# A layer norm's turn to token-major and back: 32 tensor-engine transposes, or block transposes on VectorE and a trip through HBM

## The chip, the cores and the metric

One core of a Trainium2 chip runs one program. The metric is device time in microseconds (us) of one execution; lower is better. Three runs of the kernel before gave 762.21, 762.23 and 762.68 us, median 762.23. The engines are named as in the profile: PE (tensor engine), DVE (VectorE), ACT (ScalarE), POOL (GpSimd), and SP, whose queue issues most DMAs.

## The reference, cut to what matters

A decoder layer on 512 tokens of width 1024. One of its two branches is a causal convolution over 512 channels; a layer norm and a SiLU follow, then a projection:

```
z = lax.conv_general_dilated(z, rhs, ..., feature_group_count=CONV_CH)   # width 31, depthwise
z = z + conv_b
mu = mean(z, axis=-1); var = mean((z - mu)**2, axis=-1)                  # over the 512 channels
y = (z - mu) * rsqrt(var + EPS) * ln_g + ln_b
conv_out = silu(y) @ w_conv_out
```

Beside it stand the latent attention branch, 16 blocks of gate columns (`gates = sigmoid(...)`), a merge, a cross-attention, an MLP and a last norm. Every product is computed in three matmuls from values split in a high and a low part (`hi`, `lo`).

## The kernel before, in words

Activations lie channel-major: 128 channels on the partitions, 512 tokens along them, so `acc[:, c, :]` (c = 0 to 3) holds the convolution's output. The mean over channels would run across partitions; so the norm turns `acc` to token-major (`ln[:, t, :]`, 128 tokens on the partitions, 512 channels along them), takes sum and squares per partition on ACT (L525, L530), normalises (L537), and turns back. Each turn is 16 PE transposes of 128x128 into PSUM banks, from which ACT reads (L524, L545). The way back ends in a SiLU to `acc` (L546) and the split into `yh` and `yl`, the operands of the projection `conv_out`.

The convolution's 124 taps run on DVE beside PE's matmuls: each group of three matmuls calls `tick`, which emits taps at a set rate. Around the norm PE works through the 16 gate units (`proj_unit`): each has 24 matmuls into one of four PSUM banks named `mm`; DVE then multiplies the bank by `rbx` into a scratch tile (L727) and ACT takes the sigmoid (L728). The scratch tag `sg` has two buffers, and the norm's `junk` tiles have the same tag:

```
junk = wkp.tile([P, S], F32, tag="sg", name="junk")     # in layer_norm_in
t = wkp.tile([P, S], F32, tag="sg", name="sg")          # in evac_gate
```

Weights come in chunks through two `raw` buffers, loaded by SP in the order of use: ..., gate chunk 7 (units 14 and 15), wk, wv, uq0, co0, uq1. `prep` casts a chunk or a half of it on ACT to `wh` (L202) and takes the rest on DVE or POOL to `wl` (L203); the three `wh`/`wl` buffers come free when PE has used them. POOL does it for the gate chunks.

When the convolution's generator ends, the norm isn't emitted at once: `after(D_LN1, ...)` puts its first half 10 ticks later, and `after(D_LN2, ...)` the second half 20 ticks later, each into the stream of the gate matmuls. PE's order is the program's; the other engines' order is set by a scheduler at build time and is then fixed: every engine and SP run their instructions in that order, and a waiting one holds all behind it.

Behind the gate units come, on PE: `k_pair(0)` (6 matmuls), the values `vh`, `vl` (24), `q_head(0)` (9), `q_head(1)` (9), `scores(0)`, `k_pair(1)`, `q_head(2)`, and then `conv_out`, the first reader of `yh`. ACT and DVE turn each of these banks into operands (`k`, `vh`/`vl`, `qtmp`, `q`). `k_pair(0)`'s bank is the one that `q_head(1)` takes next.

A kernel part that stands already in the program uses the operation that the change brings in: `spill`, in the MLP, turns `ht` by a DVE transpose of 32x32 blocks and four DMAs to an HBM tensor `hsp` that set the blocks in place, in runs of 32 floats (128 bytes).

Of the kernel before, what the change touches and what calls it, by code (L numbers as in the profile page):

```python
# [14 lines left out]
F32 = mybir.dt.float32  # L15
# [3 lines left out]
AF = mybir.ActivationFunctionType  # L19
# [4 lines left out]
P = 128  # L24
D = 1024
S = 512
NT = S // P
KD = D // P
CC = 512
CT = CC // P  # L30
# [135 lines left out]
D_LN1, D_LN2, D_R1, D_R2, D_M = 10, 20, 11, 8, 24  # L166


def _body(tc, a):
    nc = tc.nc  # L170
    dma = nc.sync.dma_start
    pe = nc.tensor
    dve = nc.vector
    act = nc.scalar
    gps = nc.gpsimd

    def pool(name, bufs=1, side=None, space=None):
        kw = dict(name=name, bufs=bufs, reuse_waits="tile")
        if side:
            kw["side"] = side  # L180
        if space:
            kw["space"] = space
        cm = tc.tile_pool(**kw)
        return cm, cm.__enter__()
# [11 lines left out]
    def bank(tag="mm"):  # L196
        nonlocal ps
        return ps.tile([P, S], F32, tag=tag, name=tag, bufs=PB[tag])


    def split(hi, lo, src, eng=None):
        act.copy(hi, src)  # L202
        (eng or dve).tensor_tensor(lo, src, hi.bitcast(F32), op=ALU.subtract)  # L203
# [10 lines left out]
    def after(ticks, fn):  # L214
        clock[1] += 1
        heapq.heappush(later, (clock[0] + ticks, clock[1], fn))
# [25 lines left out]
    def rsqrt(dst, v, n):  # L242
        t = sm.tile([P, n], F32, tag="rs_t", name="rs_t")
        ti = sm.tile([P, n], I32, tag="rs_i", name="rs_i")
        dve.tensor_scalar(ti, v.bitcast(I32), 1, None, op0=ALU.logical_shift_right)
        dve.tensor_scalar(dst.bitcast(I32), ti, -1, 0x5F3759DF, op0=ALU.mult, op1=ALU.add)
        for _ in range(3):
            dve.scalar_tensor_tensor(t, dst, -0.5, dst, op0=ALU.mult, op1=ALU.mult)  # L248
            dve.tensor_tensor(t, t, v, op=ALU.mult)
            dve.scalar_tensor_tensor(dst, t, 1.5, dst, op0=ALU.add, op1=ALU.mult)  # L250
# [4 lines left out]
    ident = kon[:, K_ID:K_ID + 128]  # L255
# [8 lines left out]
    def v_(name, i):  # L264
        o = VOFF[name] + i
        return vec[:, o:o + 1]
# [26 lines left out]
    sp_cm, spp = pool("spill", space=bass.MemoryType.DRAM)  # L293
# [94 lines left out]
    acc = b1.tile([P, CT, S], F32, name="acc")  # L388
# [5 lines left out]
    wk_cm, wkp = pool("wk", bufs=2, side="right")  # L394
# [91 lines left out]
    def conv_taps(c):  # L486
        run = bank("cv")
        for w in range(CW):
            zs = zpad[:, c, w:w + S]
            wcol = vec[:, w * CT + c:w * CT + c + 1]  # L490
            if w == 0:
                dve.tensor_scalar(run, zs, wcol, v_("conv_b", c), op0=ALU.mult, op1=ALU.add)
            else:
                dve.scalar_tensor_tensor(run if w < CW - 1 else acc[:, c, :], zs, wcol, run,  # L494
                                         op0=ALU.mult, op1=ALU.add)
            yield

    def conv_gen():

        started, chains = 0, []  # L500
        while started < CT or chains:
            if len(chains) < 2 and started < min(CT, zready[0]):
                chains.append(conv_taps(started))
                started += 1
            if not chains:
                yield False
                continue
            for g in list(chains):
                try:
                    next(g)  # L510
                    yield True
                except StopIteration:
                    chains.remove(g)
        after(D_LN1, layer_norm_in)

    def layer_norm_in():

        ln = tmp_.tile([P, NT, CC], F32, tag="tmaj", name="ln", bufs=1)
        s1 = sm.tile([P, NT], F32, tag="lns1", name="lns1")
        s2 = sm.tile([P, NT], F32, tag="lns2", name="lns2")  # L520
        for t in range(NT):
            b = bank(("at", "cv")[t % 2])
            for c in range(CT):
                pe.transpose(b[:, c * P:(c + 1) * P], acc[:, c, t * P:(t + 1) * P], ident)  # L524
            act.activation(ln[:, t, :], b, AF.Copy, accum_out=s1[:, t:t + 1])  # L525
        nmu = sm.tile([P, NT], F32, tag="lnm", name="lnm")
        dve.tensor_scalar(nmu, s1, -1.0 / CC, None, op0=ALU.mult)
        for t in range(NT):
            junk = wkp.tile([P, S], F32, tag="sg", name="junk")
            act.activation(junk, ln[:, t, :], AF.Square, bias=nmu[:, t:t + 1], accum_out=s2[:, t:t + 1])  # L530
        v = sm.tile([P, NT], F32, tag="rv", name="rv")
        dve.tensor_scalar(v, s2, 1.0 / CC, EPS, op0=ALU.mult, op1=ALU.add)
        r = sm.tile([P, NT], F32, tag="lnr", name="lnr")
        rsqrt(r, v, NT)
        dve.tensor_tensor(nmu, nmu, r, op=ALU.mult)
        for t in range(NT):
            act.activation(ln[:, t, :], ln[:, t, :], AF.Identity, scale=r[:, t:t + 1],  # L537
                           bias=nmu[:, t:t + 1])
        after(D_LN2, lambda: layer_norm_out(ln))

    def layer_norm_out(ln):
        for c in range(CT):
            b = bank(("at", "cv")[c % 2])
            for t in range(NT):
                pe.transpose(b[:, t * P:(t + 1) * P], ln[:, t, c * P:(c + 1) * P], ident)  # L545
            act.activation(acc[:, c, :], b, AF.Silu, scale=v_("conv_ln_g", c),  # L546
                           bias=v_("conv_ln_b", c))
            split(yh[:, c, :], yl[:, c, :], acc[:, c, :])

    conv = conv_gen()  # L550
    taps = [0.0, False]

# [201 lines left out]
    at_cm, at = pool("att", side="right")  # L754
# [87 lines left out]
    for t in range(NT):  # L842
        b = bank(("mm", "at")[t % 2])
# [715 lines left out]
```

## Time and profile before

| what | value |
|---|---|
| median of 3 runs | 762.23 us (762.21 to 762.68) |
| the profiled execution | 762.46 us, of which span 760.7 us |
| PE busy | 745.8 us, 98% of the span |
| DVE, ACT, POOL busy | 529.5 (70%), 388.5 (51%), 80.9 us (11%) |
| norm's first turn on PE (L524) | starts at 157.6 us |
| norm's second turn on PE (L545) | starts at 175.1 us |
| HBM read, written | 94.37 MB, 8.39 MB |

The profiled execution's time is 1.76 us more than its span, and 0.23 us above the median. A row of the timeline gives start, duration, engine, line, operation and out<-in; "xN" means N of them merged, and the bracket the idle time before it and what ended it. The duration of a PE matmul is longer than the distance to the next, since matmuls overlap; the distance is what counts.

### The profile page before, as it was taken

The page shows a single profiled execution, that of the slowest core. Times are in us where ns is not written, and L with a number is a line of the kernel's source. Part 1 is how long each engine was busy: PE and PEld are TensorE (multiplying, and loading weights), DVE is VectorE, ACT ScalarE, POOL GpSimd, SP SyncE. Part 2 cuts the span into 40 slices and gives each one's busy share as a digit, 9 for nine tenths or more (in the row PEclk, how much of TensorE's full clock was granted, in tenths as well). Part 3 has the DMA queues.
Part 4 walks back from the last instruction along what each step waited for, and adds up shares of the span by engine and source line. Part 5 has one row for each costly group of instructions (what it writes and reads, how often), then busy time and mean ns, then how long its engine had stood idle before and what let it go on. Part 6 is the DMA issues. An engine that isn't in the chain of part 4 may idle for free.

```text
span 760.7 us, 9482 instructions
## 1 busy us (share of the span) xinstructions
PE 745.8 (98%) x3562; PEld 620.9 (82%) x3562; DVE 529.5 (70%) x863; ACT 388.5 (51%) x657; POOL 80.9 (11%) x72
## 2 busy tenths in 40 slices
PE   8999899999999999999999999999999999999995
PEld 5889688778788887889888888888888888888884
DVE  6899999845888859856686744333333467677994
ACT  7243334468565637434475544444343566565662
POOL 0144337420000000000000000000000011111000
PEclk9999999999999999999999999999999999999998
DMA  8323124124214144423321536534353499999921
GB/s 270 124 76 133 43 79 163 56 90 139 79 28 139 57 136 151 156 86 137 111 106 61 175 89 190 150 97 184 111 204 106 138 305 263 281 221 214 247 97 56
DMA packets 40302, 105.47 MB, mean 139 GB/s; under 512 B 19264, under 2 KB 22720, under 8 KB 31296
## 3 DMA queue, kind: packets, MB, share of 16 engines
q1 hardware_dynamic: 31648, 73.84, 28.7%
q0 software_dynamic: 2944, 18.88, 12.0%
q10 hardware_dynamic: 5664, 12.15, 4.4%
q8 instruction: 28, 0.46, 0.2%
q14 instruction: 18, 0.15, 0.1%
HBM read 94.37 MB, written 8.39 MB: 135 GB/s over the span
## 4 chain that ended last, share of the span: by engine, by line
PE 79%; DVE 15%; DMA 2%; ACT 2%; issue 1%; SPq 0%; DVEq 0%
PE mm L239 21%; PE mm L237 20%; PE mm L238 20%; DVE cv L494 9%; PE at L239 4%; PE at L238 4%; PE at L237 4%; PE at L817 1%; DMA mtok<-mem 1%; PE at L798 1%; DMA xr<-xT 1%; PE at L799 1%; PE at L796 1%; DVE sg L727 1%; DVE rs_t L248 1%
## 5 line engine op out<-in xcount | busy, mean ns | idle before, releaser
L202 ACT CAST wh<-raw 128x1024 fp32r<-128x1024 f32 (+4 forms) x103 | 102.7, 998 | 170.6 <-PE mm L238 144.7
L203 DVE TENSOR_TENSOR wl<-raw,wh 128x1024 fp32r<-128x1024 f32 (+3 forms) x77 | 90.6, 1177 | 97.7 <-ACT wh L202 97.6
L237 PE MATMUL mm<-hgh,wh 128*128 128x512 f32 x288 | 112.3, 390 | 0.0
L238 PE MATMUL mm<-hgl,wh 128*128 128x512 f32 x288 | 112.1, 389 | 0.0
L239 PE MATMUL mm<-hgh,wl 128*128 128x512 f32 x288 | 112.1, 389 | 0.0
L494 DVE SCALAR_TENSOR_TENSOR cv<-zpad,vec,cv 128x512 f32<-128x512 f32 x116 | 80.4, 741 | 0.1
L237 PE MATMUL mm<-uh,wh 128*128 128x512 f32 x176 | 70.0, 398 | 3.1 <-DVE rr L250 1.6
L239 PE MATMUL mm<-uh,wl 128*128 128x512 f32 x176 | 68.8, 391 | 0.2 <-DVE wl L203 0.2
L238 PE MATMUL mm<-ul,wh 128*128 128x512 f32 x176 | 68.6, 390 | 0.0
L203 POOL TENSOR_TENSOR wl<-raw,wh 128x1024 fp32r<-128x1024 f32 (+2 forms) x26 | 56.5, 2175 | 107.3 <-ACT wh L202 97.0
L239 PEld LDWEIGHTS mm<-hgh,wl 128*128 128x128 f32 x288 | 54.1, 188 | 11.4
L238 PEld LDWEIGHTS mm<-hgl,wh 128*128 128x128 f32 x288 | 54.1, 188 | 11.1
L237 PEld LDWEIGHTS mm<-hgh,wh 128*128 128x128 f32 x288 | 54.1, 188 | 10.9
L203 DVE TENSOR_TENSOR wl<-x,wh 128x1024 fp32r<-128x1024 f32 x25 | 30.4, 1221 | 19.1 <-ACT wh L202 18.3
L1371 POOL COPY paced<-wl 128x1 f32<-128x1 f32 x4 | 2.5, 614 | 385.6 <-DVE wl L203 385.6
L237 PEld LDWEIGHTS mm<-uh,wh 128*128 128x128 f32 x176 | 33.1, 188 | 11.4 <-issue 4.1
L202 ACT CAST wh<-x 128x1024 fp32r<-128x1024 f32 x25 | 26.3, 1051 | 26.6 <-PE mm L238 9.4
L239 PEld LDWEIGHTS mm<-uh,wl 128*128 128x128 f32 x176 | 33.0, 188 | 7.7 <-DVE wl L203 0.7
L238 PEld LDWEIGHTS mm<-ul,wh 128*128 128x128 f32 x176 | 33.1, 188 | 6.4
L237 PE MATMUL at<-wh,hA 128*128 128x512 f32 x96 | 37.4, 389 | 0.0
L238 PE MATMUL at<-wl,hA 128*128 128x512 f32 x96 | 37.4, 389 | 0.0
L239 PE MATMUL at<-wh,hB 128*128 128x512 f32 x96 | 37.4, 389 | 0.0
(397 smaller groups left out, 1701.8 us busy)
## 6 DMA issues: line engine op xcount, KB each, us to landing
raw<-weights SPq DMA_DIRECT2D x42, 1024.0 KB, 4.8
x<-weights POOLq DMA_DIRECT2D x12, 1024.0 KB, 15.3
a<-weights SPq DMA_DIRECT2D x5, 1024.0 KB, 9.0
x<-weights SPq DMA_DIRECT2D x4, 1024.0 KB, 5.0
raw<-weights SPq DMA_DIRECT2D x4, 768.0 KB, 4.4
xr<-xT SPq DMA_DIRECT2D x8, 256.0 KB, 6.3
raw<-weights SPq DMA_DIRECT2D x4, 512.0 KB, 5.1
k<-kr POOLq DMA_DIRECT2D x8, 256.0 KB, 3.7
```

Of the source, the lines that this page charges most:

```text
L202: act.copy(hi, src)
L203: (eng or dve).tensor_tensor(lo, src, hi.bitcast(F32), op=ALU.subtract)
L237: pe.matmul(out, wh, ah, start=first and i == 0, stop=False, **kw)
L238: pe.matmul(out, wh, al, start=False, stop=False, **kw)
L239: pe.matmul(out, wl, ah, start=False, stop=last and i == n - 1, **kw)
L248: dve.scalar_tensor_tensor(t, dst, -0.5, dst, op0=ALU.mult, op1=ALU.mult)
L494: dve.scalar_tensor_tensor(run if w < CW - 1 else acc[:, c, :], zs, wcol, run, op0=ALU.mult, op1=ALU.add)
L727: dve.tensor_tensor(t, b, rbx, op=ALU.mult)
L796: pe.matmul(b[:, :n], q[:, 0, sl], k[:, 0, :n], start=True, stop=False)
L798: pe.matmul(b[:, :n], q[:, 0, sl], k[:, 1, :n], start=False, stop=False)
L799: pe.matmul(b[:, :n], q[:, 1, sl], k[:, 0, :n], start=False, stop=True)
L817: pe.transpose(b[:, (t - k) * P:(t - k + 1) * P], ptok[h, t][:, k * P:(k + 1) * P], ident)
```

## The change

Both turns leave PE. `turn` transposes each 128x512 tile by 32x32 blocks on DVE (two `turn` buffers), and four DMAs per tile write the blocks to their turned places in an HBM tensor (`turned`, 1 MB, one for each turn); one DMA of 1 MB then loads the turned matrix into `ln`, or into `acc`. ACT sums `ln` in place, and the SiLU reads `acc` in place. The two `after` calls are gone: both halves are emitted where the convolution ends.

```
-        after(D_LN1, layer_norm_in)
+        layer_norm_in()
+    turned = [spp.tile([S, S], F32, name="turned%d" % i) for i in range(2)]
+    def turn(tile_, dst):
+        for m in range(4):
+            t_ = wkp.tile([P, S], F32, tag="turn", name="turn", bufs=2)
+            dve.transpose(out=t_, in_=tile_(m))
+            for a_ in range(4):
+                c0 = m * P + 32 * a_
+                dma(out=dst[:, c0:c0 + 32].rearrange("(b i) j -> i b j", i=32),
+                    in_=t_[32 * a_:32 * a_ + 32, :].rearrange("i (b j) -> i b j", j=32))
...
+        turn(lambda c: acc[:, c, :], turned[0])
+        dma(out=ln, in_=turned[0].rearrange("(t p) c -> p t c", p=P))
         for t in range(NT):
-            b = bank(("at", "cv")[t % 2])
-            for c in range(CT):
-                pe.transpose(b[:, c * P:(c + 1) * P], acc[:, c, t * P:(t + 1) * P], ident)
-            act.activation(ln[:, t, :], b, AF.Copy, accum_out=s1[:, t:t + 1])
+            act.activation(ln[:, t, :], ln[:, t, :], AF.Copy, accum_out=s1[:, t:t + 1])
...
-        after(D_LN2, lambda: layer_norm_out(ln))
+        layer_norm_out(ln)
     def layer_norm_out(ln):
+        turn(lambda t: ln[:, t, :], turned[1])
+        dma(out=acc, in_=turned[1].rearrange("(c p) t -> p c t", p=P))
         for c in range(CT):
-            b = bank(("at", "cv")[c % 2])
-            for t in range(NT):
-                pe.transpose(b[:, t * P:(t + 1) * P], ln[:, t, c * P:(c + 1) * P], ident)
-            act.activation(acc[:, c, :], b, AF.Silu, scale=v_("conv_ln_g", c),
+            act.activation(acc[:, c, :], acc[:, c, :], AF.Silu, scale=v_("conv_ln_g", c),
                            bias=v_("conv_ln_b", c))
             split(yh[:, c, :], yl[:, c, :], acc[:, c, :])
```

First place: SP's queue from the last gate chunks on (the two loads of 128x1024 are wk and wv, 128x1536 are uq0 and uq1, the first 128x2048 behind uq0 is co0). A piece of the difference:

```order
 L315 DMA raw<-weights 128x1152 x2
 L315 DMA raw<-weights 128x2048 x5
+L525 DMA turned_165<-turn 32x16x32 x16
 L315 DMA raw<-weights 128x1024 x2
+L534 DMA ln<-turned_165 128x4x512
 L315 DMA raw<-weights 128x1536
 L315 DMA raw<-weights 128x2048
+L525 DMA turned_166<-turn 32x16x32 x16
 L315 DMA raw<-weights 128x1536
+L554 DMA acc<-turned_166 128x4x512
```

Sixteen stores stand ahead of wk and wv, the load of `ln` stands behind wv, and the sixteen stores of the second turn behind uq0 and co0. In the build of the changed kernel wv's load waits for POOL (its `raw` buffer is now the one of gate chunk 7), and uq0's for DVE.

Second place: ACT, from the cast of wk (`wkk`) to the keys and values of the first heads. Before:

```order
L202 CAST wkk<-raw 128x1024
L202 CAST wh<-raw 128x1024
L474 COPY csT<-at 33x512
L728 ACTIVATE gates<-sg 128x512
L525 ACTIVATE ln,lns_1430<-at 128x512
L525 ACTIVATE ln,lns_1430<-cv 128x512
L525 ACTIVATE ln,lns_1430<-at 128x512
L525 ACTIVATE ln,lns_1430<-cv 128x512
L530 ACTIVATE junk,lns_1431<-ln,lnm 128x512 x4
```

and now (the last casts of `wh` are uq0's first half, uq0's second half and co0's first half):

```order
L202 CAST wkk<-raw 128x1024
L202 CAST wh<-raw 128x1024
L536 ACTIVATE ln,lns_1374<-ln 128x512 x4
L202 CAST wh<-raw 128x768
L541 ACTIVATE junk,lns_1375<-ln,lnm 128x512 x4
L738 ACTIVATE gates<-sg 128x512 x4
L548 ACTIVATE ln<-ln,lnm,lnr 128x512 x4
L202 CAST wh<-raw 128x768
L738 ACTIVATE gates<-sg 128x512
L202 CAST wh<-raw 128x1024
L556 ACT_TABLE_LOAD
L556 ACTIVATE acc<-acc,vec 128x512 x2
```

The squares (`junk`) now stand behind uq0's first cast, four sigmoids behind the squares, and `k` and `vh` (not shown) right behind the SiLU and its `yh` casts, all behind the load of `acc`.

Third place: DVE, from the last of the norm's small instructions on. Now:

```order
L546 TENSOR_TENSOR lnm<-lnm,lnr 128x4
L522 STREAM_TRANSPOSE turn<-ln 128x512 x2
L737 TENSOR_TENSOR sg<-mm,rbx 128x512
L203 TENSOR_TENSOR wl<-raw,wh 128x768
L522 STREAM_TRANSPOSE turn<-ln 128x512
L203 TENSOR_TENSOR wl<-raw,wh 128x1024
L522 STREAM_TRANSPOSE turn<-ln 128x512
L203 TENSOR_TENSOR yl<-acc,yh 128x512 x4
L781 TENSOR_TENSOR qtmp<-mm,tq 128x512
L203 TENSOR_TENSOR k<-mm,k 64x512
L203 TENSOR_TENSOR vl<-mm,vh 128x512
L203 TENSOR_TENSOR q<-qtmp,q 128x512
```

The second turn's last transpose stands behind the split of co0's first half (128x1024), and the first `qtmp`, `k` and `vl` behind the four `yl`. Ahead of this piece, the evacuations `sg` of gate units 11 to 14 stand behind the split of uq0's first half, and each waits for ACT.

## Rows read from the trace of the kernel before

**Rows 1.** The page, shares of the chain that ended last.
```profile
PE 79%; DVE 15%; DMA 2%; ACT 2%; issue 1%; SPq 0%; DVEq 0%
```
**Rows 2.** PE's waits: engine line <- releaser: us in total, times, longest.
```profile
PE mm L237 <- DVE rr L250: 1.6, 1, 1.6
```
**Rows 3.** The chain in order of time: start us, us, what.
```profile
157.79 0.44 PE at L524 x4
...
175.29 0.44 PE at L545 x4
```
**Rows 4.** Timeline of PE: where the stretches behind the norm begin.
```profile
162.88 1.98 PE L480 MATMUL at<-csT,kon 33*128 33x512 f32 x4
...
183.01 0.39 PE L237 MATMUL mm<-ckh,wkk 128*128 128x512 f32 x1
...
189.81 0.39 PE L237 MATMUL mm<-cqh,wh 128*128 128x512 f32 x1
...
194.11 0.33 PE L796 MATMUL at<-k,q 128*128 128x128 f32 x1
...
200.42 0.39 PE L237 MATMUL mm<-yh,wh 128*128 128x512 f32 x1
```
**Rows 5.** Timeline of POOL: the last gate chunk's `wl`.
```profile
165.60 2.40 POOL L203 TENSOR_TENSOR wl<-raw,wh 128x1024 fp32r<-128x1024 f32 x1 [5.52 <-DVE rs_t L249]
```
**Rows 6.** Timeline of ACT.
```profile
159.02 0.58 ACT L525 ACTIVATE ln<-at 128x512 f32<-128x512 f32 x1
...
161.66 0.72 ACT L530 ACTIVATE junk<-ln,lnm 128x512 f32<-128x512 f32 x1 [0.24 <-DVE lnm L527]
...
164.50 1.03 ACT L202 CAST wh<-raw 128x1024 fp32r<-128x1024 f32 x1
...
169.43 2.94 ACT L537 ACTIVATE ln<-ln,lnm,lnr 128x512 f32<-128x512 f32 x4 [2.41 <-DVE lnm L535]
...
175.76 0.78 ACT L546 ACTIVATE acc<-at,vec 128x512 f32<-128x512 f32 x1 [0.63 <-PE at L545]
...
179.47 1.14 ACT L202 CAST yh<-acc 128x512 fp32r<-128x512 f32 x2
...
182.47 0.82 ACT L202 CAST wh<-raw 128x768 fp32r<-128x768 f32 x1
...
185.19 0.57 ACT L202 CAST k<-mm 64x512 fp32r<-64x512 f32 x1
```
**Rows 7.** Timeline of DVE.
```profile
147.04 0.74 DVE L494 SCALAR_TENSOR_TENSOR acc<-zpad,vec,cv 128x512 f32<-128x512 f32 x1
...
153.17 0.69 DVE L203 TENSOR_TENSOR kr<-at,kr 128x512 fp32r<-128x512 f32 x1 [0.98 <-ACT kr L202]
...
168.05 0.16 DVE L248 SCALAR_TENSOR_TENSOR rs_t<-lnr 128x4 f32<-128x4 f32 x1
...
173.34 1.22 DVE L203 TENSOR_TENSOR wl<-raw,wh 128x1024 fp32r<-128x1024 f32 x1 [2.08 <-ACT wh L202]
...
180.13 1.29 DVE L203 TENSOR_TENSOR yl<-acc,yh 128x512 fp32r<-128x512 f32 x2 [0.46 <-ACT yh L202]
```
**Rows 8.** The tile `spill`, 429 to 437 us: durations ns min/median/max, first and last start.
```profile
L1261 DVE STREAM_TRANSPOSE spill<-ht x2: 668/686/703, 429.8 to 430.5; 128x512 f32<-128x512 f32 x2
```
**Rows 9.** Timeline of SP: the first four stores of `spill`.
```profile
430.56 1.97 SPq L1264 DMA_DIRECT2D hsp<-spill  x4
```
**Rows 10.** The tile `hsp`, 432 to 433 us: the fourth of these stores.
```profile
DMA to landing us min/median/max: 2.0/2.0/2.0
```
**Rows 11.** Stretches while they move: PE, PEld, DVE, ACT, POOL busy, PEclk, DMA share, GB/s.
```profile
431.50:432.00 0.50, 0.50 (x4) 0.42 (x3) 0.15 (x1) 0.50 (x2) 0.00 (x0) 1.00 0.84 125
```
**Rows 12.** The page, DMA issues: KB each, median us to landing.
```profile
raw<-weights SPq DMA_DIRECT2D x42, 1024.0 KB, 4.8
...
raw<-weights SPq DMA_DIRECT2D x4, 512.0 KB, 5.1
...
hsp<-spill SPq DMA_DIRECT2D x32, 64.0 KB, 5.2
```
**Rows 13.** Stretches at the program's end, columns as in the group before last.
```profile
752.00:753.00 1.00, 0.90 (x4) 0.40 (x3) 0.06 (x1) 0.00 (x0) 0.00 (x0) 1.00 1.03 385
...
756.00:757.00 1.00, 0.00 (x0) 0.00 (x0) 0.46 (x1) 0.70 (x1) 0.00 (x0) 0.67 0.00 0
```
**Rows 14.** Timeline of PE at the program's start: eight warm-up matmuls of 512 columns.
```profile
1.32 3.59 PE L404 MATMUL at<-zeros 128*128 128x512 bf16 x8 [1.32 <-POOL halfpi L425]
```

## The prediction

> **What bounds the kernel now.** First the chain's shares: 79% PE, 15% DVE [rows 1]. Then PE's waits: the longest in the whole program is 1.6 us [rows 2]. So PE sets the time: what leaves PE's stream shortens the program, and what makes PE wait lengthens it by as much. Third, the chain in order of time around the norm: each turn stands on it as four groups of four transposes, 0.44 us each [rows 3]. Last, PE's timeline gives the distances [rows 4]: from the first `k_pair` matmul (183.01) to the first of `q_head(0)` (189.81) are 30 matmuls, 6.80 us, so 0.227 us each; a gate unit of 24 is 5.44 us. The first `scores` matmul starts at 194.11, the first `conv_out` matmul, reader of `yh`, at 200.42. The norm has its result well before it is read; the question is whether a longer way still has.
>
> **What is removed.** 32 transposes: 8 x 0.44 = 3.5 us of PE's chain [rows 3]; the ACT reads remain, from SBUF. If nothing else came, 762.46 - 3.5 = 759.0.
>
> **First turn, added.** The transposes cost DVE 0.7 us each [rows 8]. The first two slip among the last taps, the other two come behind them; the fourth stands behind `kr`, which ends at 153.9 [rows 7], and so ends near 154.6. Convolution and taps end about 1.4 us later than 147.8 [rows 7]; no PE work waits for that, as gate units cover it. Each tile's four stores take 1.97 us of SP [rows 9] and land 2.0 us after issue [rows 10], so the turned matrix lies in HBM by 159. Contended, stores took 5.2 us [rows 12]: 162. Neither decides: by the order, SP must first issue wv's load, which waits for POOL's `wl` of the last gate unit. That ran from 165.60 for 2.40 us [rows 5]. Its input is a cast that waits for unit 12 to free a buffer; unit 12 ended at 162.88, where L480 begins [rows 4], and now ends 1.74 us earlier, at 161.1. Cast 1.03 [rows 6], POOL 2.40: 164.6. So `ln`'s load is issued at 165.0. 1 MB takes 4.8 us alone [rows 12], with the 512 KB in front of it I take 5.5: `ln` is there at 170.5, 11.5 us later than the 159.02 of before [rows 6].
>
> Behind the load, on ACT: four sums at 0.58 = 2.3 [rows 6], to 172.8. Next in its order is uq0's first cast, which needs the `wh` buffer of gate unit 14. Unit 14's end: 183.01 - 5.44 (unit 15) - 2 x 1.74 = 174.1. Cast 0.82 to 174.9, four squares at 0.72 [rows 6] to 177.8. On DVE the evacuations of units 11 to 14 stand behind that cast's split, and the first also needs a scratch buffer of the squares: it starts when the third square ends, 177.1, and ends at 177.8. PE has filled four banks with units 11 to 14, and unit 15 takes unit 11's. So PE waits from 174.1 to 177.9, 3.8 us. This eats the 3.5 us removed: unit 15 ends at 183.3 instead of 183.0.
>
> **Second turn, added.** DVE after the squares: eleven small operations at 0.16 and a gap, say 0.2 [rows 7], three evacuations at 0.69, and hand-overs to ACT: 4.6 us, to 182.4. Four normalisations, 2.94 [rows 6]: the first done at 183.2, the last at 185.4. Transposes one and two follow to 184.6, then unit 15's evacuation and uq0's second split to 187.2 and the third transpose to 187.9 (its buffer is free when the first's stores have landed, 187.5). The fourth stands behind the split of co0. The cast for it takes the `wh` buffer of wv, so it waits for the last value matmul: 183.3 + 6.8 = 190.1. Cast 1.03, split 1.22 [rows 7], transpose 0.7: 193.1. Its four stores: last issue 1.5 us later, landing 2.0 us behind it, 196.7. The load of `acc` waits for all stores; it shares the queues with uq1, issued just ahead: 4.8 us, 201.6.
>
> **The new wait.** ACT stands at the SiLU until 201.6, and behind it, in its order, stand `k` and all of `vh`. SiLU, `yh` and the rest took from 175.76 to 180.61 [rows 6], 4.85 us: to 206.4. The last `yl` ends 0.8 us behind (181.42 against 180.61) [rows 6, 7]: 207.2. Then DVE, at 0.68 each: `qtmp`, `k`, `vl`, `q`, `k`'s other half, to 210.6. PE has run dry at 183.3 + 8.8 = 192.1, behind `q_head(0)`: `q_head(1)` wants the bank of `k_pair(0)`, which that last split frees. Nine matmuls, 2.0 us, and `scores(0)` starts at 212.7 instead of 194.11 [rows 4]: 18.6 us late. Nothing behind it gives that back, as PE hardly waits there [rows 2]. In this sum the gain of 3.5 is already used.
>
> **The clock.** At the end, the last matmul ends at 752.9, and the granted clock has fallen to half from within 756 to 757 [rows 13]. PE's new idle time, 192.1 to 210.6, is far longer, so it starts again at the lower level, 1.2 GHz. What that costs the trace shows once, at the start from rest: eight matmuls of 512 columns in 3.59 us [rows 14], where at 0.227 they are 1.82, so 1.8 us. Bounds: 0 (covered by waits for ACT) and 6.3 (the stretch from 194.11 to 200.42 at half speed, once more its length). I take 1.8, the one row.
>
> **Sum.** 18.6 + 1.8 = 20.4; 762.46 + 20.4 = 782.9, on the profiled execution, which lies 0.23 above the median. I say 783.
>
> **What is unsure.** The load of `acc`, of rows of 2 KB, has no row like it: I bound it by 3 us (1 MB at the 385 GB/s of [rows 13], 2.7, and little else) and 9 (about twice the 4.8), so -2 to +4. The fourth transpose and its stores: -4.5, if PE's values ran earlier because unit 15 found a bank (no stall at 174.1), to +3.2, if stores take 5.2 instead of 2.0 [rows 10, 12]. The stall at 174.1, 3.8 us, nears the 3.8 us behind which the clock fell in [rows 13]: 0 to +1.8. `scores(0)` also waits for a POOL transfer of `k`'s rotary rows, which may only start when `acc` is read out: 207.2 plus a few us is before 212.7, or up to +3. With the clock's bounds that is -8 to +17 about 783 if all fell on one side.
>
> **A rule against this change.** Four stores in runs of 128 bytes moved 125 GB/s with the queues 84% busy [rows 11], 64 KB in 0.5 us. The Trainium skill, "VectorE: DVE Perf Modes", section "The three transpose paths", calls a plain DMA copy that transposes by strides a trap, 19 times slower than the transposing path. So a turn's 1 MB moves in 16 x 0.5 = 8 us. The trace speaks for the row, because `spill` is the same pattern: DVE has turned the elements, and the DMA only places blocks. By the rule, 19 times the 2.7 us that 1 MB takes at 385 GB/s would be some 50 us for each turn, an estimate from that page.
>
> **Rivals.**
> - *Both trips hide* (not slower): the gate units cover both, and only the 32 transposes go: 759.0. For it: the result is read only at 200.42. It decides if `acc` lands before ACT wants to cast `k`, by about 180, 22 us before my 201.6. Against it: `ln`'s load can't be issued before 164.6. 4%; 1% that it comes out level.
> - *A milder wait*: the second turn meets a faster chain, with unit 15 unstalled, a load of 3 us and the clock's cost covered: 783 - 4.5 - 2 - 1.8 = 775. Below 772 it gets only if ACT's and DVE's hand-overs shrink besides. 6% for less than 772.
> - *Contended stores*: 5.2 us instead of 2.0 wherever a tile waits for them (the second turn's third and fourth, 6.4), half clock at both stalls (+1.8), the load at 9 (+4): 795. For it: weight chunks and 32 stores share SP's queue. 8% for above 795.
> - *One store at a time*: if a store moved on only when the one before had landed, a turn would take 16 x 2.0 = 32 us instead of 10, 22 more; the first hides 6 of that (159 against 165): 783 + 16 + 22 = 821. Against it: the four of `spill` were issued in 1.97 us and landed 2.0 each [rows 9, 10]. 2%. By the rule that the Trainium skill gives ("VectorE: DVE Perf Modes", "The three transpose paths") it would be some 42 more on each turn, 861, an estimate by that page alone.
> - *Mine*, 772 to 795: 79%.
>
> **How the numbers follow.** 783; range 772 to 795, which leaves out 4 + 1 + 6 below and 8 + 2 above, about 2 in 10. A difference under 0.2% (1.5 us) can't be told from no change here. Faster 4%, same 1%, slower 95%.
>
> **What would show it.** In the profile after: no L524 and L545 on PE; `ln`'s load issued right behind POOL's last `wl`, near 165; the squares on ACT from about 175; a PE wait of 3 to 4 us near 174, ended by an evacuation L737; the last block transpose behind a 128x1024 split near 193; ACT idle some 9 us until the load of `acc`, near 201; PE idle 15 to 20 us from about 192, its releaser DVE's `k` split, and half the granted clock behind it; from `conv_out` on, everything shifted by one amount. Wrong would be: PE without an idle time above 5 us; `acc` landing before 195; an order of waits in which `ln` was late for its stores and not for wv; or a shift that shrinks again later.

## The result, and the profile after

The changed kernel takes 785.13 us (median of 4 runs, 784.63 to 787.42), the kernel before 762.36 (4 runs, 762.21 to 762.68): ratio 1.0304, 95% interval 1.0292 to 1.0317, slower by 22.8 us. Forecast: 783, 772 to 795. The profiled execution has a span of 783.3 (before: 760.7).

PE's share of the chain has gone down, DMA's has gone up, compare [rows 1]; by line, the two loads from HBM are on it now, with 1% each:

```profile
PE 76%; DVE 16%; DMA 3%; ACT 2%; issue 1%; SPq 0%; POOL 0%; DVEq 0%; POOLq 0%
```

PE's waits (engine line <- releaser: us in total, times, longest). Above the 1.6 of [rows 2] there are two new ones, of 18.3 and 3.6 us:

```profile
PE mm L237 <- DVE qtmp L781: 18.3, 1, 18.3
PE mm L237 <- DVE sg L737: 4.5, 2, 3.6
PE mm L237 <- DVE rr L250: 1.6, 1, 1.6
```

PE's timeline at the places of [rows 4]: unit 15 behind the first wait, `k_pair(0)`, the last matmul of `q_head(0)`, `q_head(1)` behind the second wait, `scores(0)`, the first reader of `yh`.

```profile
177.87 0.80 PE L237 MATMUL mm<-uh,wh 128*128 128x512 f32 x1 [3.60 <-DVE sg L737]
...
186.27 0.39 PE L237 MATMUL mm<-ckh,wkk 128*128 128x512 f32 x1
...
194.88 0.39 PE L239 MATMUL mm<-cqh,wl 128*128 128x512 f32 x1
...
213.54 0.79 PE L237 MATMUL mm<-cqh,wh 128*128 128x512 f32 x1 [18.27 <-DVE qtmp L781]
...
217.55 0.31 PE L806 MATMUL at<-k,q 128*128 128x128 f32 x1
...
223.57 0.39 PE L237 MATMUL mm<-yh,wh 128*128 128x512 f32 x1
```

`scores(0)` comes 23.44 us late (194.11), the first `yh` 23.15 (200.42), the end 22.6: all of it is lost between 174 and 218, and 0.8 us is given back.

SP's queue shows both trips: 16 stores, two weight loads, the `ln` load; 16 stores, a weight load, the `acc` load.

```profile
145.67 10.88 SPq L525 DMA_DIRECT2D turned<-turn  x16
156.64 8.37 SPq L315 DMA_DIRECT2D raw<-weights  x2
165.24 0.38 SPq L534 DMA_DIRECT2D ln<-turned  x1
...
183.44 14.73 SPq L525 DMA_DIRECT2D turned<-turn  x16
198.26 0.45 SPq L315 DMA_DIRECT2D raw<-weights  x1
199.88 0.38 SPq L554 DMA_DIRECT2D acc<-turned  x1
```

The second of the two weight loads waits for POOL's last `wl` (162.25 + 2.38 = 164.63), and `ln` is issued behind it:

```profile
162.25 2.38 POOL L203 TENSOR_TENSOR wl<-raw,wh 128x1024 fp32r<-128x1024 f32 x1 [3.52 <-ACT wh L202]
```

ACT: the first sum behind the `ln` load, the first square, co0's cast, the SiLU behind the `acc` load, and `k`, which [rows 6] has at 185.19:

```profile
171.69 0.63 ACT L536 ACTIVATE ln<-ln 128x512 f32<-128x512 f32 x1 [1.95 <-DMA ln<-turned]
...
174.88 0.72 ACT L541 ACTIVATE junk<-ln,lnm 128x512 f32<-128x512 f32 x1
...
193.27 1.05 ACT L202 CAST wh<-raw 128x1024 fp32r<-128x1024 f32 x1 [5.44 <-PE at L239]
...
207.08 1.52 ACT L556 ACTIVATE acc<-acc,vec 128x512 f32<-128x512 f32 x2 [11.46 <-DMA acc<-turned]
...
211.99 0.57 ACT L202 CAST k<-mm 64x512 fp32r<-64x512 f32 x1
```

DVE: the evacuation of unit 11, whose last 1.17 us of waiting were for a square's scratch buffer; the last block transpose, behind co0's split; and `qtmp`, the read of `q_head(0)`'s bank:

```profile
177.13 0.69 DVE L737 TENSOR_TENSOR sg<-mm,rbx 128x512 f32<-128x512 f32 x1 [1.17 <-ACT junk L541]
...
195.50 0.70 DVE L522 STREAM_TRANSPOSE turn<-ln 128x512 f32<-128x512 f32 x1
...
212.80 0.68 DVE L781 TENSOR_TENSOR qtmp<-mm,tq 128x512 f32<-128x512 f32 x1
```

Stretches (columns as in [rows 11]): the granted clock, last but two, falls inside the first wait and again inside the second, and is at half (1.2 GHz) when PE goes on.

```profile
176.50:177.50 1.00, 0.00 (x0) 0.00 (x0) 0.37 (x1) 1.00 (x3) 0.00 (x0) 0.79 0.00 0
178.00:179.00 1.00, 1.00 (x3) 0.81 (x4) 1.00 (x4) 0.86 (x2) 0.00 (x0) 0.50 0.00 0
...
198.00:199.00 1.00, 0.00 (x0) 0.00 (x0) 0.00 (x0) 0.00 (x0) 0.00 (x0) 0.50 0.82 118
...
215.00:216.00 1.00, 1.00 (x4) 0.81 (x3) 0.97 (x2) 1.00 (x3) 0.00 (x0) 0.50 0.00 0
```

### The profile page after: what moved, and what is told of

It reads as the page before. It is cut to its first block, busy times and chain, and to the rows that moved or that the text cites. A ratio compares the mean times of both kernels' runs of the same rounds, so it can differ in the third digit from the quotient of the medians.

```text
span 783.3 us, 9480 instructions
## 1 busy us (share of the span) xinstructions
PE 747.6 (95%) x3530; PEld 621.2 (79%) x3530; DVE 531.1 (68%) x871; ACT 388.0 (50%) x656; POOL 80.8 (10%) x72
## 4 chain that ended last, share of the span: by engine, by line
PE 76%; DVE 16%; DMA 3%; ACT 2%; issue 1%; SPq 0%; POOL 0%; DVEq 0%; POOLq 0%
PE mm L239 20%; PE mm L237 20%; PE mm L238 20%; DVE cv L494 9%; PE at L239 4%; PE at L238 4%; PE at L237 4%; PE at L827 1%; DMA acc<-turned 1%; PE at L808 1%; DMA ln<-turned 1%; DMA xr<-xT 1%; DVE sg L737 1%; PE at L806 1%; PE at L809 1%
## 5 line engine op out<-in xcount | busy, mean ns | idle before, releaser
L238 PEld LDWEIGHTS mm<-hgl,wh 128*128 128x128 f32 x288 | 54.1, 188 | 11.1
```

Of the source, the lines that this page charges most:

```text
L238: pe.matmul(out, wh, al, start=False, stop=False, **kw)
```

## The experiments

A trip is here one turn by way of HBM: block transposes, stores, their landing, the load. Theory: a trip costs by what stands in line with it, in ACT's, DVE's and SP's order, and not by its length. Rivals: one trip makes all of the cost; the length itself does; the clock does.

**One trip each.** First the second turn alone goes through HBM (`e1_out_only`), then the first alone (`e2_in_only`). The other turn is again eight groups of PE transposes:

```
e1:  - layer_norm_in()            + after(D_LN1, layer_norm_in)
     - turn(acc, turned[0]); dma(out=ln, in_=turned[0])
     + pe.transpose(b[...], acc[...], ident)
e2:  - layer_norm_out(ln)         + after(60, lambda: layer_norm_out(ln))
     - turn(ln, turned[1]); dma(out=acc, in_=turned[1])
     + pe.transpose(b[...], ln[...], ident)
```

> First turn on the tensor engine as in the kernel before, second turn through HBM as in the changed one. Theory (the two trips cost apart: the first a 3.6 us wait for a bank at unit 15 with half a unit at the lower clock, the second the 18.3 us dry stretch ahead of q_head(1)): the wait at unit 15 is gone, unit 15 ends some 5 us earlier, the trip back starts earlier by as much, a wait of 8 to 18 us stays between q_head(0) and q_head(1): 773 us (771 to 778). Rival A (the price is that of the first trip; the second only waits for what the first made late): 763 to 766. Rival B (the end is set by the trip back alone, and its length doesn't depend on the first): 783 to 786.

> First turn through HBM as in the changed kernel, second on the tensor engine behind unit 15 as in the kernel before. Theory: the 3.6 us wait at unit 15 and the lower clock behind it stay (4.5 to 7 us together), the dry stretch of 18.3 us is gone: 768 us (766 to 771). Rival A (the first trip is what costs): 778 to 786. Rival B (the first trip is hidden by itself): 761 to 763.

Measured: 774.11 (773.82 to 774.59), +11.8 us, ratio 1.0156 (1.0140 to 1.0171); and 772.50 (771.05 to 774.89), +10.2, ratio 1.0137 (1.0114 to 1.0159). Together 22.0, of the 22.8 of both. The first is as expected; PE's longest wait in it:

```profile
PE mm L237 <- DVE qtmp L782: 12.6, 1, 12.6
```

The second is 4.5 us above what I expected, and outside of my range. The wait at unit 15 and the half clock behind it are there. But the edit's 60 ticks also put the transposes of the way back behind unit 15, at 186.09 (the normalised tiles are complete only at 184.6; the kernel before had them at 175.13, ahead of unit 15), and PE waits for what follows in several places:

```profile
PE mm L237 <- DVE sg L738: 4.5, 2, 3.6
PE at L807 <- ACT q L202: 2.4, 1, 2.4
...
PE at L237 <- ACT acc L557: 1.2, 1, 1.2
PE mm L637 <- ACT uh L206: 1.1, 2, 0.6
PE mm L237 <- ACT acc L557: 1.1, 1, 1.1
```

Both rivals of one guilty trip fall: each costs some 10 to 12, the first trip with its transposes back at that place, which wasn't varied.

**The scratch.** `e3_scratch` gives the squares' scratch its own tag.

```
- junk = wkp.tile([P, S], F32, tag="sg", name="junk")
+ junk = wkp.tile([P, S], F32, tag="lnj", name="junk")
```

> The changed kernel, with the scratch tile of the squares under a tag of its own, so that the evacuations of units 11 to 14 no longer share its buffers with the squares that wait for the ln load. Theory (unit 15 waits because these evacuations wait for a buffer that the squares hold): the 3.6 us wait at unit 15 is gone or under 1 us and no stretch of unit 15 is at the lower clock; unit 15 ends 4 to 6 us earlier; the dry stretch ahead of q_head(1) begins earlier and ends as the acc load allows, which starts earlier only as far as the squares do (0 to 3 us): 782 us (779 to 785). Rival (ScalarE's own order, the sums and squares ahead of the evacuations' work, makes the wait, not the buffers): the wait at unit 15 stays at 3 us or more, and 784 to 786.

Measured: 781.71 (781.55 to 781.77), ratio 1.0255 (1.0238 to 1.0272). The 3.6 us wait is gone, and so is the half clock of unit 15; so the shared scratch made it. It did so through the order more than as a wait for a buffer: with a tag of its own the squares' scratch lets the build put unit 11's evacuation on DVE at 155.68, where it stood at 177.13, behind uq0's split too:

```profile
155.68 0.69 DVE L737 TENSOR_TENSOR sg<-mm,rbx 128x512 f32<-128x512 f32 x1 [1.45 <-PE mm L239]
```

Of the 3.6 and the 2.96 that unit 15 lost to the clock (8.40 us in place of 5.44) only 3.4 come back, since PE only runs dry sooner. What comes back is about what `acc` came sooner (SiLU at 203.23, not 207.08): its load was issued 2.0 us sooner and took 5.4 us, not 7.2.

```profile
PE mm L237 <- DVE qtmp L781: 20.8, 1, 20.8
```

**The queue of the first load.** `e4_ln_pool`:

```
- dma(out=ln, in_=turned[0]...)      # SyncE's queue
+ gps.dma_start(out=ln, in_=turned[0]...)
```

> The changed kernel with the ln load issued from GpSimd's DMA queue, not behind the wv load of SyncE's queue. Theory (the load starts at 165.2 because the queue ahead of it waits for GpSimd's last low part of wv): it starts up to 2 us earlier, the sums and squares end earlier by as much, the wait at unit 15 falls to 1 to 2 us, which is short enough to keep the clock, and the trip back starts 2 to 5 us earlier: 780 us (777 to 783). Rival A (the load waits for the last of the 16 stores anyway, whatever its queue): 784 to 786. Rival B (GpSimd's queue issues later, behind its casts): 786 to 790.

Measured: 785.07 (783.34 to 785.57), as the changed kernel. A miss. The time is rival A's, but not for its reason, since the stores had landed by 160: in GpSimd's own order the load stands behind that same last `wl`. It is issued 0.96 us sooner, takes 7.8 us to land and is there no earlier:

```profile
164.28 0.96 POOL L534 DMA_DIRECT2D ln<-turned  x1
```

**The clock.** `e5_clock` keeps PE busy with 72 matmuls of zeros in the 18.3 us in which it had run dry; `e13_clock85` does it with 85.

```
+ for _ in range(72):
+     pe.matmul(wb2, identb, wide, start=True, stop=True)
  q_head(hq, 1)
```

> The changed kernel with 72 matmuls of zeros (128x512, bf16, into a bank that nobody reads) between q_head(0) and q_head(1), so that TensorE is busy in the dry stretch. Theory (the dry stretch costs its own length and then some 2 us more, because the first nine or so matmuls behind it run at 0.427 in place of 0.227): q_head(1) starts at the same time as in the changed kernel and runs at the full clock at once: 783 us (782 to 784), 2 us less. Rival (the lower clock is hidden, since the work behind waits for other things): 785.

> As the run with 72 matmuls of zeros, with 85 of them: there they ended at 209.3, 3.0 us before q_head(1) could start at 212.35, and the granted clock was at 0.50 again for its first 3.3 us. At 0.218 each, 85 end at 212.2. Theory (the lower clock behind the dry stretch has a price of its own): q_head(1) starts within 0.3 us of 212.4 with the granted clock at 1.00, its nine matmuls take 2.0 in place of 4.0, and the rest moves up by that: 781.5 us (780.5 to 782.5). Rival (the work behind q_head(1) waits for VectorE and ScalarE anyway): 783.4 as with 72.

Measured: 783.38 (783.02 to 784.48), ratio 1.0276 (1.0259 to 1.0293); and 785.19 (783.17 to 785.50), ratio 1.0295 (1.0278 to 1.0312), above both of its expectations. The first hit the expected time for another reason: unit 15 lost less to the clock and `acc` was there 1.2 us sooner. The matmuls ended 3.0 us too early, and `q_head(1)` ran at half speed as before.

```profile
212.35 0.79 PE L237 MATMUL mm<-cqh,wh 128*128 128x512 f32 x1 [3.01 <-DVE qtmp L783]
```

With 85 the clock stayed at 1.00:

```profile
213.59 0.50 PE L237 MATMUL mm<-cqh,wh 128*128 128x512 f32 x1
```

From the start of `q_head(1)` to the first `yh` it is 8.76 us then, 10.03 in the changed kernel, 8.57 in the kernel before (191.85 to 200.42): the restart costs about 1.3 us. In this execution `ln` took 8.0 us to land, not 6.4, and the wait at unit 15 was 5.17 us, which ate that; the timed runs can't tell the two kernels apart. So by the clock of the second wait alone no more than 1 to 2 of the 22.8 us are explained.

**ACT's order.** `e6_late_silu` writes the SiLU right ahead of the code that reads `yh`, and keeps `acc` in a pool that lasts until there.

```
- acc = b1.tile([P, CT, S], F32, name="acc")
+ acc = yp.tile([P, CT, S], F32, name="acc")
...
+ def silu_out():
      for c in range(CT):
          act.activation(acc[:, c, :], acc[:, c, :], AF.Silu, ...)
...
  scores(0)
  proj(2)
+ silu_out()
```

> The changed kernel with the four SiLU activations and their splits written behind scores(0) and proj(2), right ahead of the part of the program that reads y; the normalized array keeps its place until then. Nothing of the two trips is altered. Theory (what stops TensorE for 18 us is ScalarE's order: it waits at the first SiLU for the acc load and holds back k, vh and q, which the attention needs, and not the array itself): q_head(1) no longer waits at q_head(0)'s bank; a shorter wait for the acc load, which still lands at 207, stays further on, ahead of q(1)'s split or of the output projection; 775 us (770 to 779). Rival (the array is needed at that place anyway, the order only names the waiter): 783 to 786.

Measured: 780.97 (779.19 to 782.66), ratio 1.0242 (1.0225 to 1.0259); the profiled execution is the shortest of the four (779.19, span 777.4). `k`, `vh` and `q` now come ahead, and no PE wait is over 3.6 us. The gain is 4 in place of 10: the first `yh` comes at 211.54, 12 us earlier, but one SiLU still stands ahead of `q(1)`, ACT loads its tables twice more (1.28 us each), the granted clock is 0.50 from 200 to 206, and `vh` waits 2.9 us for stores of the way back, as it lies where their tiles lay (with the tiles elsewhere, in the three runs ordered by hand below, it doesn't wait).

```profile
205.22 0.81 ACT L558 ACTIVATE acc<-acc,vec 128x512 f32<-128x512 f32 x1 [5.02 <-DMA acc<-turned]
```

**All three, and the load on ACT's queue.** `e8_act` joins the scratch, four `turn` buffers, the late SiLU, and `act.dma_start` for `ln`.

> The changed kernel with both turns still through HBM and all three edits at once: scratch of the squares under its own tag, four buffers in place of two for the turned tiles, SiLU written late as in the run on that alone, and the ln load issued from ScalarE's DMA queue, so that it stands behind no weight load. Theory (the trips cost only by what stands in line with them; their own length, some 40 us, fits beside the gate units): ln lands near 165, the squares end near 176, no wait at unit 15, the four back transposes near 179 to 182, acc lands at 190 to 194, SiLU behind k, vh and q at 195, before y is read (200): 761 us (758 to 766). Rival A (the trip back is too long whatever the order): a wait of over 5 us is left ahead of the output projection, 767 to 775. Rival B (ScalarE waits at the load's issue for the stores and holds back casts that TensorE needs): a new wait at units 11 to 14, over 770.

Measured: 778.88 (776.72 to 779.90), ratio 1.0211 (1.0194 to 1.0228). None of the three expectations: the load stands on ACT behind the gates of unit 13, 12 us after the stores have landed, and `vh` waits for the last store.

```profile
169.69 0.63 ACT L740 ACTIVATE gates<-sg 128x512 f32<-128x512 f32 x1 [5.87 <-DVE sg L739]
169.98 0.38 ACTq L534 DMA_DIRECT2D ln<-turned  x1
...
198.28 0.58 ACT L202 CAST vh<-mm 128x512 fp32r<-128x512 f32 x1 [8.36 <-DMA turned<-turn]
```

So the order of each engine had to be given, not the source line alone. `behind(x)` issues a block's instructions on x's engine behind x; in short form:

```
+ put["sp"] = dma(out=ln, in_=turned[0]...)
+ with behind("sp"):    dma(out=t[:, :n], in_=src)       # all later weight loads
+ with behind("act"):   hlv = prep(("wv",), cols=512)    # act: last square
+ with behind("act", "lnm"):   evacuation of unit 13     # lnm: -mean
+ with behind("norm", "tp"):   evacuations of units 14, 15; prep_q(0)
+ with behind("norm"):  k_pair(0)     # norm: last normalising; tp: last back transpose
+ silu_out()                # behind q_head(1)
+ with behind("silu"):  scores(0)
+ junk = wkp.tile(..., tag="lnj", bufs=1)    # scratch of the squares
+ t_ = yp.tile(..., tag="turn", bufs=4)    # way back: not where vh lies; first turn: 4 in wkp
+ (gps.dma_start if a_ % 2 else dma)(out=dst...)         # way back: two queues
```

> Both turns through HBM as in the changed kernel, with the order around them written by hand: the ln load stands in SyncE's queue right behind the stores and ahead of the two weight loads that wait for GpSimd; on ScalarE the sums and squares stand ahead of the gates of units 13 to 15 and of wv's cast, the normalizing ahead of the gates of units 14 and 15; on VectorE the four back transposes stand ahead of the evacuations of units 14 and 15; the scratch has its own buffer, the turned tiles of the way back four buffers that the attention's tiles don't overlap; half of the stores of the way back go through GpSimd's queue; the SiLU stands behind q(1) and ahead of the exponentials of scores(0). Theory (the cost is order alone; the trips' own length fits beside the gate units): ln lands by 165, squares end by 172, back transposes by 180, acc lands by 192, SiLU by 201, waits of 0 to 5 us are left ahead of the output projection, TensorE has 3.5 us less work: 761 us (757 to 767). Rival (trips through HBM cost some us whatever the order): a wait of over 8 us is left ahead of the output projection or at units 13 to 15, 768 to 776.

Measured (`e10_order`): 779.82 (778.16 to 780.08), ratio 1.0227 (1.0213 to 1.0241). `ln` was there at 163, the squares ended at 170, the back transposes at 177.7, no wait at unit 15. But the way back was lost on GpSimd's queue, which neither expectation had: a store there every 2.5 us or more, and the three rope copies into `k` behind them, for which `scores(0)` waited.

```profile
PE at L830 <- DMA k<-kr: 11.0, 1, 11.0
```

```profile
195.02 0.65 POOL L538 DMA_DIRECT2D turned<-turn  x1 [1.89 <-issue]
197.57 0.66 POOL L538 DMA_DIRECT2D turned<-turn  x1 [1.90 <-issue]
198.22 1.60 POOL L819 DMA_DIRECT2D k<-kr  x3
```

`e11_order_sp` puts those stores back on SyncE's queue, and the casts of `k_pair(1)` and `q_head(2)` behind the SiLU.

> As the run before with the order written by hand, with two things altered: all sixteen stores of the way back go through SyncE's queue again (GpSimd's took 2.5 us each there, and the three rope copies into k stood behind them until 198.2), and the casts of k_pair(1) and q_head(2) stand behind the SiLU on ScalarE. Theory (the cost of the change is order alone): stores issued 175.6 to 185, acc load issued at 187 and landing at 193 to 195, rope copies at 182, no wait at scores(0), SiLU and splits from 194 to 201, a wait of 0 to 4 us at the first matmul on y, which comes at 197 to 201 (200.4 in the kernel before): 760 us (757 to 765). Rival (a fixed price of the trips): a wait of over 8 us is left, 768 to 777.

Measured: 765.82 (763.96 to 768.26), ratio 1.0055 (1.0042 to 1.0069). The median is 0.8 us above my range. Both turns go through HBM, and of the 22.8 us 19.3 are gone. SP, ACT and PE (span 762.0):

```profile
176.05 11.72 SPq L538 DMA_DIRECT2D turned<-turn  x16
187.87 0.45 SPq L328 DMA_DIRECT2D raw<-weights  x1
190.54 0.38 SPq L567 DMA_DIRECT2D acc<-turned  x1
```

```profile
196.01 1.52 ACT L571 ACTIVATE acc<-acc,vec 128x512 f32<-128x512 f32 x2 [1.70 <-DMA acc<-turned]
```

```profile
191.62 0.33 PE L833 MATMUL at<-k,q 128*128 128x128 f32 x1 [0.21 <-DVE q L206]
...
198.09 0.49 PE L240 MATMUL mm<-yh,wh 128*128 128x512 f32 x1 [0.73 <-ACT yh L205]
```

Until `scores(0)` PE is 3.2 us ahead of the kernel before (194.83 for the same matmul), nearly the 3.5 of the transposes. That goes again behind it: SiLU and splits, done by 181 before [rows 6], now stand on ACT from 193 to 201, with the exponentials behind them to 204, and PE waits for `yh`, `yl` and `p` (1.0, 0.5 and 1.7 us), 3.2 in all. The span is 1.3 us longer than before besides; where that is lost isn't shown.

`e12_two_queues` tries to win that back: half of the stores of the way back go to ScalarE's queue, and the later work of ACT is ordered behind them. In this build the SiLU comes ahead of `q(0)` in ACT's order.

```
- dma(out=dst...)
+ (act.dma_start if a_ >= 2 else dma)(out=dst...)     # way back; st: the last on ACT
+ with behind(..., "st"):  evacuations of units 14, 15; k_pair(0); prep_q(0)
```

> As the run before (order by hand, all stores on SyncE's queue), with half of the sixteen stores of the way back issued from ScalarE's queue and so no 0.73 us each on SyncE's alone, and SiLU allowed ahead of q(0) and q(1) where the array is there in time. Theory (what is left above the kernel before is the last stretch of the trip back, which ends 1.7 us after ScalarE is ready for it, and the exponentials behind it): stores issued 176 to 182, acc load issued at 184 and landing at 190, no wait at y or at the transposes of p, 3 us less than the run before: 761 us (758 to 764), the kernel before or a little under it. Rival A (the stores are bound by the DMA engines, not by issue): they land as late as with one queue, 764 to 768. Rival B (the wait of ScalarE at its own stores holds back uq0's casts and the k and v splits): a wait of over 2 us at q_head(0), 766 or more.

Measured: 768.41 (768.08 to 769.10), ratio 1.0078 (1.0064 to 1.0092). No gain from the second queue: the stores of the way back landed in 3.9 (SP) and 3.8 us (ACT, both medians), and the `acc` load was issued at 189.92, 0.6 sooner. That is rival A as far as the DMA engines were full while the stores moved. In the two idle microseconds ahead of it the load waited for the last stores, issued at 182.1 (SP) and 182.3 (ACT), which took 7.4 and 7.3 us to land; why they landed so long behind the engines' last traffic stays open.

```profile
SPq L568 <- DMA turned<-turn: 7.3, 1, 7.3
```

```profile
176.00:180.00 4.00, 4.00 (x19) 3.31 (x18) 2.71 (x5) 1.37 (x2) 0.00 (x0) 1.00 1.15 296
...
188.00:190.00 2.00, 2.00 (x11) 1.65 (x10) 1.97 (x4) 1.98 (x4) 0.00 (x0) 1.00 0.04 4
```

Rival B has a part as well: ACT stood 5.8 us at its own stores, and cast `k` at 184.95, 3.3 us later than in `e11_order_sp` (181.62), though `q_head(0)` had no long wait. That the SiLU came ahead of `q(0)` and waited for `acc` until 195.5 made a wait of 6.0 us at `scores(0)`, which hides what the queues might have given. No version beat the kernel before.

## Why the prediction was right, and where it was off

*The first turn, first load.* Right in its place: transposes done at 154.55 (154.6), POOL's `wl` at 164.63 (164.6), `ln` issued at 165.24 (165.0). The load took 6.4 us, not 5.5; that is hidden, since uq0's `wh` cast, next on ACT, waits for unit 14 until 174.1 anyway. Squares from 174.88 (175). `e10_order` bears out that its place in the queue held it: ahead of the weight loads it was issued at 157.44 and landed in 5.6 us, and the sums end 8 us sooner. (That the wait at unit 15 doesn't come there has a second reason, the scratch with its own buffer.)

*The stall at unit 15.* 3.6 us against 3.8, with its releaser; `e3_scratch` shows that the shared scratch made it. But the clock: I had put 0 to 1.8 us on it as unsure and nothing into the sum, and had read [rows 13] too long: a mean of 0.67 over 756 to 757, between 1.00 and 0.50, puts that fall near 756.3 (an estimate), not the 756.7 of my 3.8 us. Unit 15 ran 8.40 us, 2.96 too long, and `k_pair(0)` began at 186.27, not 183.3. This is the largest term that was mis-sized.

*The second turn.* The last transpose ended at 196.2, 3.1 later than forecast, nearly all of it from unit 15; the last stores landed in about 2 us, as taken (the median of this turn is 2.1, the longest 5.9). The `acc` load took 7.2 us, not 4.8 (within my 3 to 9).

*The new wait.* ACT stood at the SiLU for 11.46 us, `k` and `vh` behind it; `e6_late_silu` shows that this order made the 18.3 us, and that something else then waits. One step failed: `q_head(1)` went on behind `qtmp`, the read of `q_head(0)`'s bank, at 213.5, and not behind `k`'s second split (215.30 + 0.69). So it didn't have to wait for `k_pair(0)`'s bank, other than said ahead of the prediction. From the `acc` load to `scores(0)` that made 10.5 us, the clock included, where I had 11.1 + 1.8: 2.4 given back.

*The sum.* 3.0 (clock at unit 15) + 0.2 (stores) + 2.3 (load) - 2.4 (bank) = 3.1 above the forecast shift of 20.4 at `scores(0)`; 0.8 of it came back further on. So 785 against 783 is part luck: errors of 2.3 and 2.4 cancel.

*The restart.* 1.3 to 1.5 us by the run with 85 matmuls against the 1.8 taken.

*The rule on strided copies.* The Trainium skill, "VectorE: DVE Perf Modes", section "The three transpose paths", has a plain DMA copy that transposes by strides 19 times slower than the transposing path when the innermost stride of the destination is large; my estimate from that page was some 50 us a turn. That case isn't this one: DVE has turned the elements, and the DMAs place blocks, in runs of 128 bytes. Here 32 such stores landed in 2.0 us (median), and a turn was in HBM some 13 to 16 us behind its first store, much of which was waiting for transposes. No run here has a copy that turns elements by strides.

*Not settled.* In the hand-ordered kernel the profiled execution is the shortest of five (763.96; up to 768.26). What the others lose isn't known.

## What to carry to other kernels

Work that leaves the busiest engine is paid for in the queues of the others: for each new wait, write down what stands behind it in that engine's order and in that DMA queue, and whose buffers it holds. Here 19 of 23 us were such order and shared buffers, and they went only when the order was given on SP, ACT and DVE together; a single mend left the wait or moved it to the next engine. A last part stays: the result came too late for ACT's spare time, and 3.2 us won on PE were lost there again.

## What the runs showed that I had not expected

- The clock behind a wait of 3.6 to 3.9 us is not the same from run to run. Unit 15, 24 matmuls, took 8.40 us in the changed kernel, 7.99 in `e4_ln_pool`, 7.19 in `e5_clock`, and 5.59 in `e6_late_silu`, where the clock never fell though PE had waited as long:

```profile
177.63 0.50 PE L237 MATMUL mm<-uh,wh 128*128 128x512 f32 x1 [3.60 <-DVE sg L739]
```

```profile
178.00:179.00 1.00, 1.00 (x6) 0.82 (x5) 1.00 (x4) 0.86 (x2) 0.00 (x0) 1.00 0.00 0
```

  Whether that makes the scatter of the kernels with this wait (1.5 to 3.8 us over their runs) is open: `e3_scratch`, without it, scatters by 0.2, but `e8_act` and `e11_order_sp`, without it too, by 3.2 and 4.3.
- The 1 MB `acc` load landed in 5.4 to 5.5 us in four kernels and in 7.2 to 7.6 in six. In the six a weight load was issued 1.6 to 2.1 us ahead of it, in the four none, or one 2.7 us ahead. In `e10_order`, behind the rope copies, it took 8.3. That they share the engines is the plain reading; it wasn't tried alone.
- GpSimd's queue took 2.5 us for a store of 64 KB (0.65 and a gap of 1.89 for which the profile shows no reason), SyncE's 0.5 to 0.7.
